# A hybrid encoder layer on one core: V's tiles at multiples of 64 bytes, the last row pair by halves in fresh banks, four reciprocals behind a weight chunk's low parts

## The chip, the cores and the metric

The kernel runs on one core of one Trainium2 chip. The metric is the device time of one execution in microseconds (us); the time before is 630.35 us, the median of 3 runs (630.19 to 630.4). Engines in the profile: PE (TensorE, matmuls), PEld (its weight loads), DVE (VectorE), ACT (ScalarE), POOL (GpSimd) and SP, which here only issues transfers. A q behind an engine's name (SPq, ACTq) means its sequencer, with the transfers it issues.

## The reference

One layer of a bidirectional encoder, 512 tokens of 2048 features: a combined input projection, attention (8 heads of 128, 2 key/value heads, axial rotary embedding) beside a gated linear recurrence in both directions, both normed and gated, and one output projection with the residual.

```
h = rms_norm(x, norm_w)
proj = jnp.einsum('bsd,de->bse', h, w_in)
q, k, v, g_attn, xr, g_lru = jnp.split(proj, SPLITS, axis=-1)
attn_out = attention_group(q, k, v, q_norm_w, k_norm_w)
lru_out = lru_group(xr, conv_w, conv_b, lru_wa, lru_ba, lru_wx, lru_bx, lru_lambda)
mixed = jnp.concatenate([rms_norm(attn_out, attn_norm_w) * jax.nn.silu(g_attn),
                         rms_norm(lru_out, lru_norm_w) * jax.nn.silu(g_lru)], axis=-1)
return x + jnp.einsum('bse,ed->bsd', mixed, w_out)
```

## The kernel before

**Products in three parts.** Every operand of a matmul is split into a high part (a rounded copy, fp32r) and a low part (what is left), and a product is three matmuls: high by high, high by low, low by high (`mm3`, L152 to L155, and `product`, L1029, for the output projection). ScalarE makes the high parts (for weights L218), VectorE the low parts (L219). So each 256-row chunk of the input projection's weights (`wload`, L224) comes through a ring of three raw buffers, and gives two pairs of high and low tiles, k = 0 and 1, of 128x512. `wsplit` (L211) numbers the chunks in `turn_of` and keeps, in `split_done`, the two instructions (the copy, the subtraction) of the chunk's k = 1 under the chunk's number. A chunk is used by 24 matmuls: four output blocks, each two k by three.

**Order.** TensorE's order is written out by hand. For the other engines most of the program is ordered by a planner, by priority (`tc.high_priority`), its own estimate of when things are ready, and the edges that the program gives it: `tc.issue_after(ins)`, wrapped in `behind(those)` (L243), puts an instruction behind another on the same engine. SP is ordered by hand in the attention stage, and all four other engines are in the output projection (`outputs`).

**V and attention.** `kv` (L654) takes keys and values from the projection. For each of 4 token blocks one V tile holds the high and the low part, 256 columns each (2 heads of 128). The tile is made by `aside` (L863): it is 16 columns of 4 bytes longer than needed, 2112 bytes per partition, and V begins 8 columns (32 bytes) in. V's parts are the stationary operand of `values` (L731): 12 matmuls per head, with the softmax weights (tiles ph and pl) as moving operand. There are eight heads.

**The norm's reciprocals.** `spread` (L827) sums squares over partitions by two matmuls with ones, ScalarE takes the square root into `gbc`, and VectorE inverts it in place in four pieces of 128 columns (L835). It is called twice: for the recurrence (from `kv`) and for attention (from `later`, L1351, after the first two output blocks of the last input projection, with high priority). That last projection takes its chunks by `take` (L1300), which fetches one chunk more and hands over the oldest of those fetched; three are fetched ahead.

**The output projection.** It uses a form of Strassen's method with seven products of half-size blocks, named P1, Q5, Q6, Q7, Q3, P2, Q4, for each half g of the output columns, each a sum over NP = 8 steps i. `product(dst, i, k, b, n)` adds step i to the two PSUM banks dst[0] and dst[1], one for each block of 128 rows (s), in six matmuls of 512 columns. The last three products (Q3, P2, Q4) run together; in the second half their last two steps are drawn apart at the end, L1139: first both steps of Q3, then of P2, then of Q4, and after each product `last` (L1060) adds its two banks to the result tiles xt and cb in SBUF (VectorE, L1066) and sends the rows out (L1058). For the very last product, Q4, the second row block's add is cut into two halves, the first sent by ScalarE's queue, the second by SP's. In the loop over i before it, `feed` issues loads and splits of the output weights for later steps, on VectorE among others, and `residual` (L1103) adds x (L1112).

Of the kernel before, what the change touches and what calls it, by code (L numbers as in the profile page):

```python
# [12 lines left out]
F32R = mybir.dt.float32r  # L13
# [4 lines left out]
P = 128  # L18
SEQ = 512
DM = 2048  # L20
KT = DM // P
NT = SEQ // P
HD = 128
NH = 8
NKV = 2
# [23 lines left out]
H = 256  # L49
# [14 lines left out]
def hybrid_kernel(  # L64
# [53 lines left out]
    def nm(s):  # L118
        cnt[0] += 1
        return f"{s}_{cnt[0]}"  # L120
# [19 lines left out]
    def pj():  # L140
        return ps.tile([P, SEQ], F32, tag="pj", name=nm("pj"))
# [101 lines left out]
    def behind(those):  # L243
        stack = ExitStack()
        for ins in those:
            stack.enter_context(tc.issue_after(ins))
        return stack
# [406 lines left out]
    def kv(es):  # L654
        turned_k = sent(norm_rope(es, NKV, rk), NKV)
        yield 20
        opened("wx", "right")
        for t in range(NT):
            vv = es[t][:, NKV * HD :]
            vt = aside(  # L660
                lambda *a: pools["qkv"].tile(*a, tag="v", bufs=NT, name=nm("v")), 2 * NKV * HD // H
            )
            vh[t], vl[t] = vt[:, 0, :], vt[:, 1, :]
            nc.scalar.copy(vh[t], vv)
            nc.vector.tensor_sub(vl[t], vv, f(vh[t]))
        yield from lru_squares()
        yield 2
        drain(turned_k)
        yield 6
        pair = landed(asides.pop(0))  # L670
        for h in range(NKV):
            yield (12, 4)[h]
            kt = pools["qkv"].tile([P, 2, SEQ], F32R, tag="kt", bufs=NKV, name=nm("kt"))
            kth[h], ktl[h] = kt[:, 0, :], kt[:, 1, :]
            those = split_head(pair, h, kth[h], ktl[h])
        parts = halved(
            sums["l"],
            lambda: pools["rope"].tile([P, SEQ], F32R, tag="kv", bufs=NT, name=nm("kv")),
            those,
        )  # L680
        yield 4
        spread(gbc, parts, NB * P)
# [141 lines left out]
            nc.vector.tensor_sub(lo, src, f(hi))  # L824
        return hi, lo

    def spread(dst, parts, n):  # L827

        pb = mm()
        for k, part in enumerate(parts):  # L830
            nc.tensor.matmul(pb, ones_r, part, start=k == 0, stop=k == 1)  # L831
        nc.scalar.activation(dst, pb, AF.Sqrt, scale=1.0 / n, bias=eps[:, :1])
        for t in range(NT):
            ts_ = slice(t * P, (t + 1) * P)
            nc.vector.reciprocal(dst[:, ts_], dst[:, ts_])  # L835

    gbc = const([P, SEQ], "gbc")

# [12 lines left out]
    def seven(pair, hi, lo):  # L851
# [7 lines left out]
        for to, part in ((slice(0, 3), src[:, 1:4]), (slice(3, 7), res)):  # L859
            nc.scalar.copy(hi[:, to], part)  # L860
            nc.vector.tensor_sub(lo[:, to], part, f(hi[:, to]))

    def aside(tile_of, n):  # L863

        t = tile_of([P, n * H + 16], F32R)
        return t[:, 8 : 8 + n * H].rearrange("p (n e) -> p n e", e=H)

    def kept(pool, i):
        return [
# [144 lines left out]
    def outputs(work):  # L1014

        order = [(g, n, i) for g in range(2) for n in range(2) for i in range(NP)]
        feeds, parts = [], []  # L1020
        for g, n, i in order:
            parts.append([])
            feeds.append((feed1, feed2)[n](g, i, parts[-1]))

        def feed(u):
            if u < len(feeds):
                next(feeds[u])

        def product(dst, i, k, b, n):  # L1029
            ah, al = (t[:, k] for t in mixed[i][1])  # L1030
            bh, bl = (t[:, n] for t in b)
            for s in range(2):
                ts_ = slice(s * P, (s + 1) * P)
                for j, (lh, rh) in enumerate(((ah, bh), (ah, bl), (al, bh))):
                    nc.tensor.matmul(  # L1035
                        dst[s], lh[:, ts_], rh, start=i == 0 and j == 0, stop=i == 7 and j == 2
                    )

        def banks(*kinds):
            return [[kind() for _ in range(2)] for kind in kinds]  # L1040

        with tc.high_priority(SOON):
            for u in (0, 1, 0, 0, 1):
                feed(u)
        next(work)
        feed(1)
        next(work)
        feed(2)
        for g in range(2):

            xs = [
                pools["out"].tile([P, NT, SEQ], F32, tag=t, bufs=1, name=nm(t))
                for t in ("xt", "cb")
            ]

            def leave(t, j, queue, e0=0, e1=SEQ):
                c0 = (2 * g + j) * SEQ
                queue.dma_start(of[tokens[t], c0 + e0 : c0 + e1], xs[j][:, t, e0:e1])  # L1058

            def last(t0, j, acc, cut=1):  # L1060
                for s in range(2):
                    n = cut if s else 1
                    for e0 in range(0, SEQ, SEQ // n):
                        e1 = e0 + SEQ // n
                        to = xs[j][:, t0 + s, e0:e1]
                        nc.vector.tensor_add(to, to, acc[s][:, e0:e1])  # L1066
                        queue = nc.scalar if e1 < SEQ else nc.sync
                        leave(t0 + s, j, queue if g else nc.gpsimd, e0, e1)

            p1, q5, q6, q7 = banks(*((mm, mm, pj, pj), (pj, mm, mm, pj))[g])  # L1070
            for i in range(NP):
                u = 16 * g + i
                xb, yb = parts[u]
                product(p1, i, P1, xb, 1)
                if i < NP - 1:
                    product(q5, i, Q5, xb, 0)
                    next(work, None)
                    feed(u + 2)
                    product(q6, i, Q6, yb, 0)
                    product(q7, i, Q7, yb, 1)  # L1080
                    feed(u + 2)
                    feed(u + 3)
                    continue

                for s in range(2):
                    nc.scalar.copy(xs[1][:, 2 + s], p1[s])
                product(q6, i, Q6, yb, 0)
                for s in range(2):
                    nc.vector.tensor_sub(xs[1][:, s], xs[1][:, 2 + s], q6[s])
                product(q5, i, Q5, xb, 0)  # L1090
                for s in range(2):
                    nc.vector.tensor_sub(xs[0][:, 2 + s], q5[s], xs[1][:, s])
                feed(u + 2)
                product(q7, i, Q7, yb, 1)
                for s in range(2):
                    nc.vector.tensor_add(xs[0][:, s], q7[s], xs[0][:, 2 + s])
                feed(u + 2)
                for s in range(2):
                    nc.vector.tensor_sub(xs[1][:, s], xs[1][:, s], q7[s])
                feed(u + 3)  # L1100


            def residual(m, j):  # L1103
                xr = in_av() if g else in_fin("t4", 2, 2)
                c0 = (2 * g + j) * SEQ
                nc.gpsimd.dma_start(
                    xr,
                    xf[2 * m * P : 2 * (m + 1) * P, c0 : c0 + SEQ].rearrange("(t p) e -> p t e", p=P),
                )
                yield  # L1110
                to = xs[j][:, 2 * m : 2 * m + 2]
                nc.vector.tensor_add(to, to, xr)  # L1112
                if (m, j) == (0, 0):
                    for t in range(2):
                        leave(t, 0, nc.gpsimd)
                yield

            rs = [residual(n // 2, n % 2) for n in range(4)]
            next(rs[0]), next(rs[1])
            q3, p2, q4 = banks(*((mm, mm, pj), (pj, mm, mm))[g])  # L1120
            takes = ((q3, Q3, 0, 0), (p2, P2, 0, 1), (q4, Q4, 1, 0))
            ends = ((2, 0), (2, 1), (0, 1))
            added = (2, 3, 4, 5) if g else (2, 3, 5, 6)
            for i in range(NP - 2 * g):
                u = 16 * g + NP + i
                for (dst, k, b, n), (t0, j) in zip(takes, ends):
                    product(dst, i, k, parts[u][b], n)
                    if i == NP - 1:
                        last(t0, j, dst)
                    if k == P2:  # L1130
                        if i in added:
                            next(rs[added.index(i)])
                        if i in (2, 3):
                            next(rs[i])
                        feed(u + 2)
                feed(u + 2)
                feed(u + 3)

        for (dst, k, b, n), (t0, j) in zip(takes, ends):  # L1139
            for i in (NP - 2, NP - 1):  # L1140
                product(dst, i, k, parts[24 + i][b], n)
            last(t0, j, dst, 2 if k == Q4 else 1)

# [205 lines left out]
    def later():  # L1351
# [1 line left out]
            parts = halved(sums["a"], lambda: fin_s(dt=F32R))  # L1353
        yield 2
        with tc.high_priority():
            spread(gbc, parts, NH * HD)
        yield 4
        for pair in ap_[:2]:
            normed(pair)
# [86 lines left out]
```

## Time and profile before

| | |
|---|---|
| median of 3 runs | 630.35 us |
| the profiled execution's own time | 630.30 us |
| its span, first to last instruction | 628.2 us |
| granted TensorE clock | 0.999 |
| matmuls, and their weight loads | 2755 each |
| DMA, mean over the span | 203 GB/s |

The profile's tables give for a group: line, engine, operation, out<-in tiles, shape, count, then busy time in us, mean of one in ns, and idle time before. The timeline gives the start in us, the time taken in us, engine, line, operation, tiles, shape and count (several in a row are merged). A wait row says who waited for whom: total us, how often, longest. Matmuls overlap: one is recorded for about 0.39 us, but the next starts 0.23 us after it, and it is the distance of starts that sets the time.

### The profile page before, as it was taken

The numbers are of one execution on the slowest core, as the hardware profiler recorded it, in microseconds if no ns is written. First come the engines' busy times: TensorE is split into PE (matmuls) and PEld (weight loads), VectorE is DVE, ScalarE is ACT, GpSimd is POOL, SyncE is SP. The second block draws the span as 40 slices with busy tenths as digits, with TensorE's granted clock in tenths as the row PEclk, the third lists the DMA queues.
The fourth block names the chain that finished last, engine by engine and source line by source line (L and its number), as shares of the span: only waits on it lengthen the run. The fifth ranks groups of instructions, "written<-read, shape, count | busy, mean of one in ns | idle before, by whom it ended". The sixth has DMA issues, their size and how long they took to land.

```text
span 628.2 us, 8273 instructions
## 1 busy us (share of the span) xinstructions
PE 622.0 (99%) x2755; PEld 512.5 (82%) x2755; DVE 494.6 (79%) x794; ACT 353.1 (56%) x618; POOL 101.4 (16%) x134
## 2 busy tenths in 40 slices
PE   9999999999999999999999999999999999999997
PEld 7888888888888888888888888887888888888885
DVE  5958979986699875987887888549978866886885
ACT  3674899379946823555475447438436643444441
POOL 0000210112002622522122232100120101110010
PEclk9999999999999999999999999999999999999999
DMA  8878785859774599479668646922996777896252
GB/s 284 281 209 263 176 202 172 176 134 192 237 234 135 172 255 227 109 214 267 183 170 254 194 150 185 268 69 67 280 232 204 224 254 244 287 340 213 68 201 100
DMA packets 73594, 127.61 MB, mean 203 GB/s; under 512 B 6616, under 2 KB 29264, under 8 KB 73552
## 3 DMA queue, kind: packets, MB, share of 16 engines
q1 hardware_dynamic: 65664, 109.65, 55.9%
q0 software_dynamic: 7712, 17.31, 14.2%
q8 instruction: 21, 0.34, 0.2%
q14 instruction: 21, 0.17, 0.1%
q10 hardware_dynamic: 176, 0.14, 0.1%
HBM read 110.29 MB, written 37.75 MB: 236 GB/s over the span
## 4 chain that ended last, share of the span: by engine, by line
PE 98%; DVE 1%; issue 0%; DVEq 0%; POOL 0%; POOLq 0%
PE pj L155 20%; PE pj L153 20%; PE pj L154 20%; PE mm L1035 14%; PE pj L1035 10%; PE mm L155 4%; PE mm L153 3%; PE mm L154 3%; PE pj L388 1%; PE mm L253 1%; PE mm L1153 1%; DVE gbc L835 1%; DVE wl L219 0%; DVE cb L1066 0%; PE mm L831 0%
## 5 line engine op out<-in xcount | busy, mean ns | idle before, releaser
L155 PE MATMUL pj<-x,wl 128*128 128x512 f32 x376 | 146.8, 390 | 0.4 <-DVE wl L219 0.3
L153 PE MATMUL pj<-x,wh 128*128 128x512 f32 x376 | 147.0, 391 | 0.0
L154 PE MATMUL pj<-x,wh 128*128 128x512 f32 x376 | 146.6, 390 | 0.0
L218 ACT CAST wh<-wr 128x512 fp32r<-128x512 f32 x143 | 85.4, 617 | 81.9 <-PE pj L154 32.0
L219 DVE TENSOR_TENSOR wl<-wr,wh 128x512 fp32r<-128x512 f32 x144 | 100.0, 724 | 21.2 <-ACT wh L218 19.9
L887 ACT CAST wh<-wr 128x1024 fp32r<-128x1024 f32 (+1 forms) x72 | 60.5, 860 | 77.3 <-PE mm L1035 35.9
L888 DVE TENSOR_TENSOR wl<-wr,wh 128x1024 fp32r<-128x1024 f32 (+1 forms) x72 | 68.5, 985 | 30.7 <-ACT wh L887 30.5
L155 PEld LDWEIGHTS pj<-x,wl 128*128 128x128 f32 x376 | 70.6, 188 | 16.1 <-DVE wl L219 1.3
L153 PEld LDWEIGHTS pj<-x,wh 128*128 128x128 f32 x376 | 70.6, 188 | 14.7
L154 PEld LDWEIGHTS pj<-x,wh 128*128 128x128 f32 x376 | 70.6, 188 | 14.7
L153 PE MATMUL pj<-wh,x 128*128 128x512 f32 x192 | 74.8, 389 | 0.0
L155 PE MATMUL pj<-wh,x 128*128 128x512 f32 x192 | 74.8, 389 | 0.0
L154 PE MATMUL pj<-wl,x 128*128 128x512 f32 x192 | 74.8, 389 | 0.0
L911 POOL DMA_DIRECT2D t<-in_w_out_dram x40 | 33.5, 901 | 161.3 <-DMA t<-in_w_out_dram 99.5
L1035 PE MATMUL mm<-wl,mh 128*128 128x512 f32 x128 | 49.8, 389 | 0.0
L1035 PE MATMUL mm<-wh,mh 128*128 128x512 f32 x128 | 49.8, 389 | 0.0
L1035 PE MATMUL mm<-wh,ml 128*128 128x512 f32 x128 | 49.8, 389 | 0.0
L153 PEld LDWEIGHTS pj<-wh,x 128*128 128x128 f32 x192 | 36.0, 188 | 7.5
L154 PEld LDWEIGHTS pj<-wl,x 128*128 128x128 f32 x192 | 36.0, 188 | 7.5
L155 PEld LDWEIGHTS pj<-wh,x 128*128 128x128 f32 x192 | 36.0, 188 | 7.4
L708 POOL TENSOR_SCALAR p<-p,sm 128x512 f32<-128x512 f32 x32 | 24.3, 764 | 90.0 <-DVE sm L707 90.0
L1035 PE MATMUL pj<-wh,mh 128*128 128x512 f32 x96 | 37.4, 390 | 0.0
(200 smaller groups left out, 1038.2 us busy)
## 6 DMA issues: line engine op xcount, KB each, us to landing
wr<-in_w_in_dram SPq DMA_DIRECT2D x71, 512.0 KB, 5.1
wr<-in_w_out_dram SPq DMA_DIRECT2D x24, 512.0 KB, 5.1
t<-in_w_out_dram POOLq DMA_DIRECT2D x40, 256.0 KB, 6.8
wr<-t SPq DMA_DIRECT2D x40, 256.0 KB, 5.9
pd<-u SPq DMA_DIRECT2D x16, 512.0 KB, 3.0
pt<-pd SPq DMA_DIRECT2D x64, 128.0 KB, 3.9
t<-in_w_out_dram SPq DMA_DIRECT2D x24, 256.0 KB, 5.5
t<-t SPq DMA_DIRECT2D x16, 256.0 KB, 5.7
```

The costliest lines, as they stand in the source:

```text
L153: nc.tensor.matmul(acc, lh, rh, start=start, stop=False)
L154: nc.tensor.matmul(acc, lh, rl, start=False, stop=False)
L155: nc.tensor.matmul(acc, ll, rh, start=False, stop=stop)
L218: copy(hi, raw[:, k, :]).ins,
L219: nc.vector.tensor_sub(lo, raw[:, k, :], f(hi)).ins,
L253: nc.tensor.transpose(pt[:, t * P : (t + 1) * P], xc[:, t, ks], ident)
L388: nc.tensor.matmul(acc[e], w[:, e * P : (e + 1) * P], x_[k], start=k == 0 and j == 0, stop=False,)
L708: last_pool[0] = nc.gpsimd.tensor_scalar(p, p, sm, 0.0, op0=ALU.mult, op1=ALU.add).ins
L887: nc.scalar.copy(hi[:, to], b)
L888: nc.vector.tensor_sub(lo[:, to], b, f(hi[:, to]))
L911: nc.gpsimd.dma_start(dst, src, accum_op=ALU.add)
L1035: nc.tensor.matmul(dst[s], lh[:, ts_], rh, start=i == 0 and j == 0, stop=i == 7 and j == 2)
```

## The change

Three edits.

V's tile is allocated as [128, 2, 256] directly; `aside` goes. So each V tile is 2048 bytes per partition instead of 2112, and V starts where the tile starts.

`spread` takes a list `those`, and each of its four reciprocals is put behind these instructions on VectorE. The second call hands over the k = 1 subtraction of the chunk that was fetched last but one; the first call hands over nothing.

In the output projection's second half, Q4's sum for the second row block is closed after step 5 (NP - 3), and VectorE adds it to the result there (one more add of 128x512). The two last steps then run in another order: first both steps for the first row block, its add and its transfer; then, in two newly taken PSUM banks, both steps for columns 0 to 255 of the second row block, with add and transfer, and both steps for columns 256 to 511, with add and transfer. Twelve matmuls of 256 columns take the place of six of 512; the weight loads of the second row block are made twice.

```diff
         for t in range(NT):
             vv = es[t][:, NKV * HD :]
-            vt = aside(
-                lambda *a: pools["qkv"].tile(*a, tag="v", bufs=NT, name=nm("v")), 2 * NKV * HD // H
-            )
+            vt = pools["qkv"].tile([P, 2, NKV * HD], F32R, tag="v", bufs=NT, name=nm("v"))
             vh[t], vl[t] = vt[:, 0, :], vt[:, 1, :]
...
-    def spread(dst, parts, n):
+    def spread(dst, parts, n, those=()):
...
-            nc.vector.reciprocal(dst[:, ts_], dst[:, ts_])
+            with behind(those):
+                nc.vector.reciprocal(dst[:, ts_], dst[:, ts_])
...
-        def product(dst, i, k, b, n):
+        def product(dst, i, k, b, n, ss=range(2), es=slice(None), ends_=(0, NP - 1)):
             ah, al = (t[:, k] for t in mixed[i][1])
             bh, bl = (t[:, n] for t in b)
-            for s in range(2):
+            for s in ss:
                 ts_ = slice(s * P, (s + 1) * P)
                 for j, (lh, rh) in enumerate(((ah, bh), (ah, bl), (al, bh))):
                     nc.tensor.matmul(
-                        dst[s], lh[:, ts_], rh, start=i == 0 and j == 0, stop=i == 7 and j == 2
+                        dst[s][:, es], lh[:, ts_], rh[:, es],
+                        start=i == ends_[0] and j == 0, stop=i == ends_[1] and j == 2,
                     )
...
-            def last(t0, j, acc, cut=1):
-                for s in range(2):
-                    n = cut if s else 1
-                    for e0 in range(0, SEQ, SEQ // n):
-                        e1 = e0 + SEQ // n
-                        to = xs[j][:, t0 + s, e0:e1]
-                        nc.vector.tensor_add(to, to, acc[s][:, e0:e1])
-                        queue = nc.scalar if e1 < SEQ else nc.sync
-                        leave(t0 + s, j, queue if g else nc.gpsimd, e0, e1)
+            def last(t0, j, acc, ss=range(2), e0=0, e1=SEQ):
+                for s in ss:
+                    to = xs[j][:, t0 + s, e0:e1]
+                    nc.vector.tensor_add(to, to, acc[s][:, e0:e1])
+                    queue = nc.scalar if e1 < SEQ else nc.sync
+                    leave(t0 + s, j, queue if g else nc.gpsimd, e0, e1)
...
                 for (dst, k, b, n), (t0, j) in zip(takes, ends):
-                    product(dst, i, k, parts[u][b], n)
+                    if g and i == NP - 3 and k == Q4:
+                        product(dst, i, k, parts[u][b], n, (0,))
+                        product(dst, i, k, parts[u][b], n, (1,), ends_=(0, i))
+                        nc.vector.tensor_add(xs[j][:, t0 + 1], xs[j][:, t0 + 1], dst[1])
+                    else:
+                        product(dst, i, k, parts[u][b], n)
...
         for (dst, k, b, n), (t0, j) in zip(takes, ends):
-            for i in (NP - 2, NP - 1):
-                product(dst, i, k, parts[24 + i][b], n)
-            last(t0, j, dst, 2 if k == Q4 else 1)
+            pieces = [(dst, (0, 1), 0, SEQ, (0, NP - 1))]
+            if k == Q4:
+                pieces = [(dst, (0,), 0, SEQ, (0, NP - 1))] + [
+                    ((None, pj()), (1,), e0, e0 + H, (NP - 2, NP - 1)) for e0 in (0, H)
+                ]
+            for to, ss, e0, e1, ends_ in pieces:
+                for i in (NP - 2, NP - 1):
+                    product(to, i, k, parts[24 + i][b], n, ss, slice(e0, e1), ends_)
+                last(t0, j, to, ss, e0, e1)
...
         with tc.high_priority():
-            spread(gbc, parts, NH * HD)
+            spread(gbc, parts, NH * HD, split_done[turn_of[0] - 2][1:])
```

More of the change, by code (lines that the diff above doesn't have):

```diff
@@ L861, in seven @@
             nc.vector.tensor_sub(lo[:, to], part, f(hi[:, to]))
-    def aside(tile_of, n):
-        t = tile_of([P, n * H + 16], F32R)
-        return t[:, 8 : 8 + n * H].rearrange("p (n e) -> p n e", e=H)
     def kept(pool, i):
```

## The prediction

> **What bounds the kernel now.** I read the page first (engine table, chain, clock row), then TensorE's waits, then the timeline at the one place where it waits late, at V's matmuls and over the last 15 us.
>
> ```profile
> span 628.2 us, 8273 instructions
> PE 622.0 (99%) x2755; PEld 512.5 (82%) x2755; DVE 494.6 (79%) x794; ACT 353.1 (56%) x618; POOL 101.4 (16%) x134
> PEclk9999999999999999999999999999999999999999
> PE 98%; DVE 1%; issue 0%; DVEq 0%; POOL 0%; POOLq 0%
> L153 PE MATMUL mm<-kt,q 128*128 128x512 f32 x32 | 12.5, 389 | 0.0
> L153 PE MATMUL mm<-ph,v 128*128 128x512 f32 x32 | 12.7, 397 | 0.0
> PE pj L155 <- DVE wl L219: 0.3, 1, 0.3
> ```
>
> TensorE is busy 99% at full clock and is 98% of the chain; everything else has its cover. A change can only win where TensorE loses cadence or stands still, and after its last matmul. In a steady stretch 21 matmuls of 512 columns take 4.78 us (row at 618.12 below), 0.2267 us each by the finer spacing of neighbouring starts. The change touches one place of each kind: V's matmuls (mean 397 ns where others show 389), the only late wait of TensorE, and the tail.
>
> **The change part by part.** All sums start from the profiled execution's own 630.30 us: a span of 628.2 and 2.1 around it. The median of the runs, 630.35, is practically the same.
>
> *V's tiles.* Two blocks of V, the first and the last of eight (32 matmuls of a kind, four per head):
>
> ```profile
> 300.77 0.40 PE L155 MATMUL mm<-kt,q 128*128 128x512 f32 x1
> 301.01 0.39 PE L153 MATMUL mm<-ph,v 128*128 128x512 f32 x1
> 305.65 0.39 PE L155 MATMUL pj<-x,wl 128*128 128x512 f32 x1
> 416.53 0.40 PE L155 MATMUL pj<-x,wl 128*128 128x512 f32 x1
> 421.41 0.39 PE L155 MATMUL pj<-x,wl 128*128 128x512 f32 x1
> ```
>
> From the matmul during which V's first weights are loaded to the place where the old cadence is back are 21 matmuls: 12 with V as weights, one before and eight behind. They take 305.65 - 300.77 = 4.88 us, and 421.41 - 416.53 = 4.88 again, where 21 x 0.2267 = 4.76. So a block loses 0.12 us, and eight lose 0.95. The two blocks agree though different work stands before them (kt,q; pj), so the loss belongs to the V block. In the code, V is the one weight operand that begins 32 bytes inside its tile; the program's memory plan puts every other matmul operand of 128 or 512 columns at a multiple of 64 bytes. The change puts V there too. No run shows V at another address, so the gain lies between nothing and 0.95. I take **-0.95**, since the only operand placed differently is the one that is slow, in all its uses. The edit itself adds no instruction: the same four casts and four subtractions, 256 bytes less in all, so tiles allocated below V move by 256 bytes, which keeps them at multiples of 64.
>
> The Trainium skill ("SBUF — State Buffer", Specifications) speaks against this: it gives SBUF lines of 16 bytes, so a start at 32 bytes is already on a whole line, and by it the move is worth nothing. No run so far separates the two; what it would make of the sum is the first rival.
>
> *The second reciprocal.*
>
> ```profile
> 426.40 0.39 PE L153 MATMUL pj<-x,wh 128*128 128x512 f32 x1
> 432.24 1.13 ACT L218 CAST wh<-wr 128x512 fp32r<-128x512 f32 x2
> 433.85 0.95 DVE L861 TENSOR_TENSOR ml<-hs,mh 128x768 fp32r<-128x768 f32 x1
> 434.71 3.39 DVE L835 RECIPROCAL gbc<-gbc 128x128 f32<-128x128 f32 x4
> 437.98 0.39 PE L154 MATMUL pj<-x,wh 128*128 128x512 f32 x1
> 438.01 2.43 DVE L219 TENSOR_TENSOR wl<-wr,wh 128x512 fp32r<-128x512 f32 x4
> 438.70 0.50 PE L155 MATMUL pj<-x,wl 128*128 128x512 f32 x1 [0.33 <-DVE wl L219]
> 441.58 0.39 PE L155 MATMUL pj<-x,wl 128*128 128x512 f32 x1
> 444.30 0.39 PE L155 MATMUL pj<-x,wl 128*128 128x512 f32 x1
> 445.97 1.23 DVE L840 TENSOR_TENSOR av<-av,gbc 128x1024 f32<-128x1024 f32 x1
> ```
>
> The high parts of a weight chunk were ready at 433.4, but VectorE ran four reciprocals first, and the chunk's low parts came at 438.7. TensorE needed the first at 438.21 and stood; from 437.98 to 441.58 are 13 matmuls, 3.60 us against 13 x 0.2267 = 2.95. So the place costs 0.65: 0.49 of standing and the rest in slow cadence behind it. Counting chunks: when the reciprocals are written into the program, the chunk last fetched is the fourth of this projection; two back in the numbering means the third, and its second low part is what they are pinned behind. That is the chunk of the stall (chunks of 24 matmuls, 5.44 us, after the projection's start at 426.40; the two matmuls of the sums lie in between). The order becomes: two low parts from 434.8 to 436.1, ahead of 438.21; then reciprocals until 439.5; then the next chunk's two low parts, until 440.4 as before, where TensorE first asks for one at 444.30. The work on VectorE is the same, only exchanged. Late next is the reciprocals' result, 439.5 instead of 438.0, with its first reader at 445.97. The weights' raw buffers come free some 3 us earlier, which only helps SP's loads. **-0.65**; bounds 0 (the planner lets another piece of work take the place) and 0.65.
>
> *The last row pair.*
>
> ```profile
> 613.93 1.22 DVE L1112 TENSOR_TENSOR cb<-cb,wr 128x1024 f32<-128x1024 f32 x1
> 615.21 1.83 DVE L888 TENSOR_TENSOR wl<-wr,wh 128x1024 fp32r<-128x1024 f32 x2
> 617.48 1.37 DVE L1066 TENSOR_TENSOR xt<-xt,pj 128x512 f32<-128x512 f32 x2 [0.44 <-PE pj L1035]
> 618.12 4.78 PE mm L1035 x21
> 620.20 1.37 DVE L1066 TENSOR_TENSOR cb<-cb,mm 128x512 f32<-128x512 f32 x2 [1.35 <-PE mm L1035]
> 622.92 1.43 DVE L1066 TENSOR_TENSOR cb<-cb,mm 128x512 f32<-128x512 f32 x3 [1.35 <-PE mm L1035]
> 623.17 0.39 PE L1035 MATMUL mm<-wh,ml 128*128 128x512 f32 x1
> L1066 DVE TENSOR_TENSOR cb<-cb,mm 128x256 f32<-128x256 f32 x2 | 0.8, 418 | 0.0
> 623.93 0.41 DVE L1066 TENSOR_TENSOR cb<-cb,mm 128x256 f32<-128x256 f32 x1
> 624.05 0.37 ACTq L1058 DMA_DIRECT2D out_dram<-cb  x1
> 624.38 0.33 SPq L1058 DMA_DIRECT2D out_dram<-cb  x1
> GB/s 282 328 109 0 0 0 0 73 391 355 401 346 328 319 118 0 0 0 0 64 355 382 364 342 310 332 178 5 0 0 0 0 0 0 0 0 0 0 0 0
> out_dram<-cb SPq DMA_DIRECT2D x1, 128.0 KB, 2.7
> 15.78 1.03 PE L253 MATMUL mm<-ident,b 128*128 128x128 f32 x8
> L253 PE MATMUL mm<-ident,b 128*128 128x128 f32 x40 | 5.8, 287 | 0.0
> ```
>
> (The GB/s row is of the window 620 to 629, slices of 0.225 us.) Today the last adds run behind each other: the first row block at 622.92 for 0.69, two halves of 0.42, out at 624.35; the final transfer is issued at 624.38. The DMA engines are busy without a gap from slice 19 (about 624.4) to slice 26 (626.1): three transfers, 512 KB together, the last of them queued behind the other two.
>
> The change adds one VectorE add of 128x512 (0.69) in the sixth step. It stands between the two subtractions of 615.21, and waits for matmuls that end about 615.6, before its turn at 616.43. Behind it the second subtraction ends at 617.8 instead of 617.1; TensorE wants that result only at about 621.4. The two adds of 617.48 start about 0.3 late, their transfers too, and the idle 1.35 before 620.20 takes that up: nothing on the path. Cover gone, it would be 0.69.
>
> The last 12 matmuls start at 623.17 - 11 x 0.227 = 620.68. New order: six for the first row block, the last starting at 621.81 and ending at 622.20; its add 622.24 to 622.93. Then twelve of 256 columns in place of six of 512. No row has that shape. Below: half of 0.227, 0.113. Above: 0.227, no shrinking. Nearest are the eight transposes, a weight load with 128 columns each: (1.03 - 0.29) / 7 = 0.106 us, 0.29 being the mean length of one. Loading weights so fits under 0.113, and I take 0.12. The first half ends about 622.92 and is added until 623.35, the second ends at 623.64, is added by 624.09 and issued at 624.12: 0.26 earlier. From issue to first byte today's first block takes some 0.8 us (added by 623.61, bytes from slice 19 on); at 624.12 + 0.8 = 624.9 the earlier two transfers, moved forward by 0.6 to 0.7, are through, so it also saves the queueing of some 0.45 (624.38 + 0.8 = 625.2 against a start about 625.65). **-0.70**. Bounds: -0.77 at 0.113; -0.26 if landing stays 2.7 after the issue; +0.57 if the halves stay at 0.227 each (1.28 later at the add, less what was saved).
>
> Sum: 630.30 - 0.95 - 0.65 - 0.70 = **628.0**.
>
> **The rivals.**
>
> *V's start doesn't matter.* The cadence also slows behind aligned operands:
>
> ```profile
> 429.12 0.62 PE L831 MATMUL mm<-s,ones_r 128*128 128x512 f32 x2
> 430.73 0.39 PE L155 MATMUL pj<-x,wl 128*128 128x512 f32 x1
> ```
>
> From 429.12 are seven matmuls in 1.61 us, where 7 x 0.2267 = 1.59. If the V blocks' loss comes from their waits or from p as moving operand, it stays: 630.30 - 1.35 = 628.95. Against it: this place costs 0.02 to 0.03, a V block four times that. It would also be the outcome by the skill's 16-byte lines.
>
> *The stall only moves.* The planner that orders VectorE puts other waiting work (the 1.22 and 0.95 subtractions of the build) before the two low parts, enough to be late by as much: more than the 2.1 us between 436.1 and 438.2. Then -0.65 is lost: 628.65.
>
> *Halves as slow as wholes.* 630.30 - 0.95 - 0.65 + 0.57 = 629.27, within the bound below. The transposes at 0.106 speak against it.
>
> *Slower: a new plan.* Outside the last stage the planner orders VectorE and ScalarE anew, from the moved V tiles (which lie on memory of earlier tiles, and so wait for others) and the new edges on. Place: the weights' low parts from 190 to 470 us. Price: 0.65 for each chunk late, as at 438. Up to three such stalls leave the time between 628.65 and 629.95; four are needed to eat 2.30, and six give 630.30 - 2.30 + 3.90 = 631.9. For it: VectorE is busy 79%, more in these stretches. Against it: the present plan has one wait of this kind after the start (0.3 in the waits row), and the edges are in one place.
>
> **How the numbers follow.** A measurement here can tell 0.2%, 1.26 us, from no change: faster is under 629.09, slower over 631.61. All as forecast, 628.0: 0.56. V worth nothing, 628.95: 0.14. Stall moved, 628.65: 0.07. These three are faster: 0.77. Halves not shrinking, 629.27: 0.06, and a new plan with two or three stalls, about 629.6: 0.09, make "same" 0.15. The slower plan, 631.9: 0.08. The range from 627.4 (all at their best bound, and half a microsecond of slow cadence elsewhere that goes as well) to 629.4 holds the first four, 0.83.
>
> **What would show it.** V's matmuls at a mean of 389 to 391 instead of 394 to 397, and 4.76 us over the same 21; if they stay, the first rival holds. The row of TensorE waiting for L219 gone, reciprocals from about 436; a wait elsewhere on wl names the moved stall. Twelve matmuls of 128x256 over 1.36 to 1.45 us, the last issue 0.2 to 0.3 closer to TensorE's end than now (the 1.2 from 623.17 to 624.38). New idle on TensorE between 190 and 470 would make the prediction wrong.

## The result, and the profile after

| | before | after |
|---|---|---|
| median of 6 runs | 630.28 us (629.92 to 630.4) | 627.57 us (627.17 to 628.09) |
| span of the profiled execution | 628.2 us | 625.6 us |
| own time of the profiled execution | 630.30 us | 627.43 us |

The ratio is 0.9958, 95% interval 0.9946 to 0.9971: 2.7 us faster, more than the 0.2% that can be told from no change. The forecast was 628.0.

The page of the kernel after (span, engines, clock, chain):

```profile
span 625.6 us, 8287 instructions
PE 620.6 (99%) x2761; PEld 513.1 (82%) x2761; DVE 494.3 (79%) x795; ACT 353.1 (56%) x618; POOL 101.6 (16%) x134
PEclk9999999999999999999999999999999999999999
PE 99%; DVE 0%; issue 0%; POOL 0%; POOLq 0%
```

Six matmuls more and 1.4 us less of busy TensorE: what TensorE gained is cadence and standing time, not work. The rest of the gain lies behind its last matmul. The table of TensorE's waits no longer has the row of L219; what is left of it is the start:

```profile
PE mm L1156 <- POOL ones L161: 1.1, 1, 1.1
```

V's matmuls, in the table of groups (last number but one the mean in ns):

```profile
L153 PE MATMUL mm<-ph,v 128*128 128x512 f32 x32 | 12.5, 390 | 0.0
```

The first V block in the timeline, from its first start to the start of the 21st behind it:

```profile
300.42 0.39 PE L155 MATMUL mm<-kt,q 128*128 128x512 f32 x1
300.65 0.39 PE L153 MATMUL mm<-ph,v 128*128 128x512 f32 x1
...
305.18 0.39 PE L155 MATMUL pj<-x,wl 128*128 128x512 f32 x1
```

The mean went from 397 to 390 ns, and the same 21 matmuls take 305.18 - 300.42 = 4.76 us instead of 4.88.

VectorE around the second reciprocal, and TensorE's matmul that used to wait:

```profile
433.48 1.28 DVE L219 TENSOR_TENSOR wl<-wr,wh 128x512 fp32r<-128x512 f32 x2
434.68 3.38 DVE L834 RECIPROCAL gbc<-gbc 128x128 f32<-128x128 f32 x4
437.98 1.22 DVE L219 TENSOR_TENSOR wl<-wr,wh 128x512 fp32r<-128x512 f32 x2
...
436.71 0.39 PE L154 MATMUL pj<-x,wh 128*128 128x512 f32 x1
436.93 0.39 PE L155 MATMUL pj<-x,wl 128*128 128x512 f32 x1
437.16 0.39 PE L153 MATMUL pj<-x,wh 128*128 128x512 f32 x1
```

Two low parts, four reciprocals, two low parts: TensorE goes from 436.71 to 436.93 without a stop where it stood 0.49 us before.

The tail in the timeline (VectorE's adds, TensorE's last pieces, the last issue):

```profile
613.28 1.23 DVE L882 TENSOR_TENSOR wl<-wr,wh 128x1024 fp32r<-128x1024 f32 x1
614.43 0.68 DVE L1122 TENSOR_TENSOR cb<-cb,mm 128x512 f32<-128x512 f32 x1
615.02 0.69 DVE L882 TENSOR_TENSOR wl<-wr,wh 128x512 fp32r<-128x512 f32 x1
615.63 1.29 DVE L1058 TENSOR_TENSOR xt<-xt,pj 128x512 f32<-128x512 f32 x2
618.27 1.37 DVE L1058 TENSOR_TENSOR cb<-cb,mm 128x512 f32<-128x512 f32 x2 [1.35 <-PE mm L1029]
...
620.11 0.28 PE L1029 MATMUL pj<-wh,mh 128*128 128x256 f32 x1
621.42 0.28 PE L1029 MATMUL pj<-wh,ml 128*128 128x256 f32 x1
...
621.74 0.42 DVE L1058 TENSOR_TENSOR cb<-cb,pj 128x256 f32<-128x256 f32 x1 [0.30 <-PE pj L1029]
622.19 0.33 SPq L1053 DMA_DIRECT2D out_dram<-cb  x1
```

The last transfer in the table of issues (size, us from issue to landing):

```profile
out_dram<-cb SPq DMA_DIRECT2D x1, 128.0 KB, 2.3
```

Eleven distances from 620.11 to 621.42 make 0.119 us for a matmul of 256 columns. The early add (L1122) sits between the two subtractions, and the idle 1.35 before 618.27 is as long as before, so it costs nothing. From the end of the last matmul to the end of the span it is now 625.6 - 621.7 = 3.9 us; before it was 628.2 - 623.56 = 4.6.

**Where the 2.60 us of span went.** Matching TensorE's matmuls one by one in the two traces, the lead grows in four places: 0.35 in the first 50 us, 0.93 over the eight V blocks (0.12 each, but 0.09 for one that took 4.79), 0.65 at the reciprocals, and 0.67 in the tail (0.75 less after TensorE's end, 0.08 more on TensorE). The first of these is none of the change's: the kernel before stood 0.3 us for a low part at the start, where the change has no instruction. Those rows of before:

```profile
43.17 0.39 PE L154 MATMUL pj<-x,wh 128*128 128x512 f32 x1
43.66 0.50 PE L155 MATMUL pj<-x,wl 128*128 128x512 f32 x1
```

In other executions this stall is missing or lies elsewhere: the single edits below are the kernel before up to that point; two show none of that size, and the third one at 48.87. So a span from one execution carries some tenths of a microsecond from the start, and the three terms are read from their places.

### The profile page after: what moved, and what is told of

Its sections match the earlier page's. It is cut to its first block, busy times and chain, and to the rows that moved or that the text cites. A ratio compares the mean times of both kernels' runs of the same rounds, so it can differ in the third digit from the quotient of the medians.

```text
span 625.6 us, 8287 instructions
## 1 busy us (share of the span) xinstructions
PE 620.6 (99%) x2761; PEld 513.1 (82%) x2761; DVE 494.3 (79%) x795; ACT 353.1 (56%) x618; POOL 101.6 (16%) x134
## 4 chain that ended last, share of the span: by engine, by line
PE 99%; DVE 0%; issue 0%; POOL 0%; POOLq 0%
PE pj L153 21%; PE pj L155 21%; PE pj L154 21%; PE mm L1029 14%; PE pj L1029 11%; PE mm L155 3%; PE mm L153 3%; PE mm L154 3%; PE pj L388 1%; PE mm L253 1%; PE mm L1156 1%; PE mm L829 0%; PE mm L367 0%; DVE cb L1058 0%; PE mm L189 0%
## 5 line engine op out<-in xcount | busy, mean ns | idle before, releaser
L219 DVE TENSOR_TENSOR wl<-wr,wh 128x512 fp32r<-128x512 f32 x144 | 99.6, 720 | 21.3 <-ACT wh L218 20.2
L1029 PE MATMUL pj<-wl,mh 128*128 128x512 f32 (+1 forms) x100 | 38.5, 385 | 0.0
```

Of the source, the lines that this page charges most:

```text
L219: nc.vector.tensor_sub(lo, raw[:, k, :], f(hi)).ins,
L1029: nc.tensor.matmul(dst[s][:, es], lh[:, ts_], rh[:, es], start=i == ends_[0] and j == 0, stop=i == ends_[1] and j == 2,)
```

## The experiments

Times are medians; the kernel before ran on the same chip and in the same rounds (medians 630.27 to 630.29). The ratio to it, with its 95% interval, goes by all runs, so it is not exactly the quotient of two medians.

| run | median us | ratio |
|---|---|---|
| v_only | 629.17 | 0.9983 (0.9974 to 0.9992) |
| recip_only | 629.54 | 0.9989 (0.9980 to 0.9998) |
| tail_only | 629.09 | 0.9981 (0.9972 to 0.9990) |
| weights_aside | 638.48 | 1.0131 (1.0117 to 1.0144) |
| weights_64b | 635.95 | 1.0090 (1.0076 to 1.0104) |
| weights_16b | 637.60 | 1.0114 (1.0099 to 1.0130) |
| rows_only | 627.98 | 0.9963 (0.9951 to 0.9976) |
| begin12 | 629.59 | 0.9999 (0.9990 to 1.0008) |
| all_by_64 | 627.40 | 0.9956 (0.9944 to 0.9969) |
| v_64_of_2304 | 628.32 | 0.9968 (0.9955 to 0.9980) |
| v_128_of_2304 | 628.41 | 0.9970 (0.9958 to 0.9982) |
| ones_moved | 627.60 | 0.9955 (0.9941 to 0.9969) |

### Each edit alone

v_only is the kernel before with the V line of the diff; recip_only the kernel before with `those` handed to the second `spread`; tail_only is the change with the other two undone (V's tiles 2112 bytes long again, and V 32 bytes in).

> The kernel before with V's tiles moved alone. Theory (V's start 32 bytes in slows the cadence): each of eight V blocks goes from 4.88 to 4.76 us, TensorE's end comes 0.95 us earlier, time 0.9 to 1.0 under before (ratio about 0.9985); the stall at 438 and the tail stay. Rival (start doesn't matter, the blocks' loss comes from waits or from the moving operand): 4.88 us stays and the time is before's within 0.2.

> The kernel before with the reciprocals' pin alone. Theory: TensorE's only late wait on the low parts near 438 goes, 0.65 us (ratio about 0.9990); V blocks stay 4.88, the tail stays. Rival (the stall only moves, or the edges make a new plan): a wait on low parts elsewhere, time as before within 0.2.

> The change with V's start and the pin undone, so the last row pair alone. Theory: 12 matmuls of 256 columns at 0.12 us, 0.08 longer on TensorE, last issue 0.2 to 0.3 earlier, end 0.7 us earlier (ratio about 0.9989). Rival (landing takes as long from the issue as before): 0.26 earlier.

Each is faster on its own, by 1.1, 0.7 and 1.2 us; the sum, 3.0, agrees with the whole 2.7 within the intervals of about half a microsecond each. The traces are sharper. With V alone a block, from 300.33 to 305.10, takes 4.77 us, as two rows of its timeline show:

```profile
300.33 0.39 PE L155 MATMUL mm<-kt,q 128*128 128x512 f32 x1
305.10 0.39 PE L155 MATMUL pj<-x,wl 128*128 128x512 f32 x1
```

Its waits still have the stall on low parts:

```profile
PE pj L155 <- DVE wl L219: 0.4, 1, 0.4
```

With the reciprocals held back alone (recip_only) the waits table has no such row, and TensorE stands for low parts nowhere else after the start: the stall went and did not move. With the tail alone, TensorE's last matmul starts at 623.50 of a span of 627.6, as far from the end as in the change, and its last transfer lands 2.3 us after its issue, not 2.7. So each edit brings its own gain. The rivals "the stall only moves", "halves as slow as wholes" and "landing takes as long from the issue as before" fall. So does "V's start doesn't matter"; what it is about V's start that matters isn't settled by v_only, which changes both the 32 bytes and the length of the tiles.

### The suspected cost taken twelvefold: weights 32, 64 and 16 bytes in

```diff
-        hi = pool.tile([P, SEQ], F32R, tag="wh", bufs=4, name=nm("wh"))
-        lo = pool.tile([P, SEQ], F32R, tag="wl", bufs=4, name=nm("wl"))
+        hi, lo = (
+            pool.tile([P, SEQ + 16], F32R, tag=t, bufs=4, name=nm(t))[:, 8 : 8 + SEQ]
+            for t in ("wh", "wl")
+        )
```

weights_64b begins at column 16 of the same tiles, weights_16b at column 4.

> The change, with the high and low tiles of all chunks of the input projection's weights begun 32 bytes inside tiles 64 bytes longer. Theory that a weight (stationary) operand 32 bytes in costs 5.7 ns a matmul: the 1128 matmuls with these tiles as stationary operand go from a distance of 0.2267 to 0.2325, 6 to 6.5 us slower than the change, so about 634; the 576 matmuls that have these tiles as moving operand stay at 0.2267. If a moving operand counts as well: 3.3 us more, about 637. Rival (the start doesn't matter): 627.6.

> As the run before with the weights' tiles 64 bytes longer, but begun 64 bytes in instead of 32. Theory (what counts is the start within 64 bytes): cadence 0.2267 again, time as the change's, 627.2 to 628.1. Rival (the longer tiles, or where the other tiles come to lie, made the 638.5): 638 again.

> The same tiles begun 16 bytes in. If any start off a multiple of 64 bytes costs (a row of 64 bytes more to read per partition): 637 to 640, as at 32 bytes. If only the half, 32 bytes, counts, or a start at a multiple of 16 is free: 627.6.

The first came out 10.9 us over the change, more than either estimate: the mean distance of these matmuls is 0.232 to 0.233 us, about what the theory said for weights and moving operands together, and others behind them are slow too. Groups of weights_aside (stationary: pj<-x,wh; moving: pj<-wh,x; not touched: mm<-wh,mh):

```profile
L153 PE MATMUL pj<-x,wh 128*128 128x512 f32 x376 | 148.7, 395 | 0.0
L153 PE MATMUL pj<-wh,x 128*128 128x512 f32 x192 | 75.9, 395 | 0.0
L1031 PE MATMUL mm<-wh,mh 128*128 128x512 f32 x126 | 49.0, 389 | 0.0
```

So the operand's place counts when it is the moving operand as well as when it is the weights. In the moving groups the weights (x) all lie where they lay in the change, so it isn't only the step from one set of weights to the next. But then weights_64b, 64 bytes in, is slow too, and my theory falls: a multiple of 64 is not enough. Its groups:

```profile
L153 PE MATMUL pj<-x,wh 128*128 128x512 f32 x376 | 148.2, 394 | 0.0
L153 PE MATMUL pj<-wh,x 128*128 128x512 f32 x192 | 75.5, 393 | 0.0
L1031 PE MATMUL mm<-wh,mh 128*128 128x512 f32 x126 | 49.0, 389 | 0.0
```

weights_16b, 16 bytes in, is slow as well: 637.60, means of 393 to 396 ns. A cost of any start off a multiple of 64 would look like this too, but weights_64b rules that reading out.

I then took every matmul's two operands from the program's memory plan and set the distance to the next matmul beside them. In the change both operands of every matmul of 512 columns start at 192 modulo 256 bytes, except in the six that have the ones as weights. Tiles of 2112 bytes start 64 bytes further each: in the kernel before V began at 224, 32, 96 and 160 modulo 256, in weights_64b the weights begin at 0, 64, 128 and 192. The pairs that differ modulo 256 were slow in all these runs (mean distance 0.231 to 0.235 us by groups); in the change, pairs that differ by odd multiples of 256 are not (0.2267). A quarter of the weight tiles in weights_64b do lie at 192, and their matmuls are 0.230 to 0.233 us apart all the same; misplaced ones stand a few matmuls before and behind them, so this run alone doesn't give the rule. That made a new theory, that moving operand and weights have to start at the same place modulo 256, with rivals: the place itself (192), or a period of 64 or 128.

### The same place modulo 256

```diff
+    const([P, 16], "gap")
     ident = const([P, P], "ident")
...
-    opened("pad", "right").tile([P, 8], F32, name="pad")
+    opened("pad", "right").tile([P, 56], F32, name="pad")
```

(all_by_64.) For V alone, in the change, with columns 16 to 528 (v_64_of_2304) or 32 to 544 (v_128_of_2304):

```diff
-            vt = pools["qkv"].tile([P, 2, NKV * HD], F32R, tag="v", bufs=NT, name=nm("v"))
+            vt = pools["qkv"].tile([P, 576], F32R, tag="v", bufs=NT, name=nm("v"))
+            vt = vt[:, 16 : 528].rearrange("p (n e) -> p n e", e=H)
```

> The change with every SBUF tile moved by 64 bytes (modulo 256): by the memory plan all moving and stationary operands of 512 and 128 columns then start at 0 modulo 256, where in the change they all start at 192; ones stays 64 apart from the rest. Theory R (what counts is that moving operand, weights and the next weights start at the same place modulo 256): cadence 0.2267, time as the change's, 627 to 628. Theory A (the place itself counts): distances of 0.231 to 0.233 everywhere, 638 or more.

> The change with V's tiles 2304 bytes long (9 x 256) and V begun 64 bytes in: V is at a multiple of 64 bytes, at 0 modulo 256 where all other operands are at 192. Multiples of 64 suffice: 4.76 us per V block, the change's time. Same place modulo 256 counts: about 4.85 to 4.88 per block, 0.7 to 0.95 over the change.

> The same tiles with V begun 128 bytes in, 64 modulo 256. If the period is 128: 4.76 us per V block, the change's time. If it is 256: about 4.85 to 4.88, 0.7 to 0.95 over the change.

The first V block in all_by_64, then in v_64_of_2304, then in v_128_of_2304, from a matmul to the 21st behind it:

```profile
300.58 0.39 PE L154 MATMUL mm<-kt,q 128*128 128x512 f32 x1
305.34 0.39 PE L154 MATMUL pj<-x,wh 128*128 128x512 f32 x1
```

```profile
300.24 0.39 PE L155 MATMUL mm<-kt,q 128*128 128x512 f32 x1
305.11 0.39 PE L155 MATMUL pj<-x,wl 128*128 128x512 f32 x1
```

```profile
300.45 0.40 PE L155 MATMUL mm<-kt,q 128*128 128x512 f32 x1
305.33 0.39 PE L155 MATMUL pj<-x,wl 128*128 128x512 f32 x1
```

4.76, 4.87 and 4.88 us. Everything moved together to 0 keeps the full cadence (627.40), so the place itself doesn't count; V at a multiple of 64 that lies 64 from the rest, and even at one that lies 128 from it, loses what it lost 32 bytes in (0.75 and 0.84 over the change by the medians, 0.9 by the traces). Period 64 and period 128 fall. What in the chip has this period wasn't tried.

### Ones and identity to the same place

```diff
+    const([P, 16], "gap")
     ident = const([P, P], "ident")
...
+    const([P, 48], "gap2")
     nhalf = const([P, 48], "nhalf")
```

> The change with the ones and the identity, the last operands off the common place, moved to 192 modulo 256 as all others. If the same place counts: the 0.02 to 0.03 us of slow cadence behind each of the three sums over partitions go (L829 near 236 and 428, L367 near 50), under 0.1 us in all, less than the time can tell. If their cadence stays, those places have another cause.

The last sum over partitions in the timeline of the change, then of ones_moved, each to the seventh matmul behind its first:

```profile
427.84 0.62 PE L829 MATMUL mm<-s,ones_r 128*128 128x512 f32 x2
429.45 0.39 PE L155 MATMUL pj<-x,wl 128*128 128x512 f32 x1
```

```profile
428.24 0.61 PE L831 MATMUL mm<-s,ones_r 128*128 128x512 f32 x2
429.82 0.39 PE L155 MATMUL pj<-x,wl 128*128 128x512 f32 x1
```

1.61 becomes 1.58, and the other two sums do the same: the row that I had set against V's start in the prediction had the same cause as V. In the time it can't be told (627.60).

### The tail without halves

```diff
-                pieces = [(dst, (0,), 0, SEQ, (0, NP - 1))] + [
-                    ((None, pj()), (1,), e0, e0 + H, (NP - 2, NP - 1)) for e0 in (0, H)
-                ]
+                pieces = [
+                    (dst, (0,), 0, SEQ, (0, NP - 1)),
+                    ((None, pj()), (1,), 0, SEQ, (NP - 2, NP - 1)),
+                ]
```

The second row block's add is still cut in halves.

> The change, but the second row block's last six matmuls stay 512 columns wide in one new bank, and its add is in two halves at the end: the row order and the early add alone. Theory (the end is the last add plus the queue behind it): TensorE ends 0.08 earlier than the change, the last issue comes 0.3 later than the change's relative to TensorE's end, as in the kernel before, but the first row block's transfer is out of the way; time 0.2 to 0.4 over the change's 627.57. Rival (halves bring nothing, the earlier first transfer is all): the change's time.

Its last matmul and the two last adds in the timeline:

```profile
621.60 0.39 PE L1029 MATMUL pj<-wh,ml 128*128 128x512 f32 x1
622.02 0.75 DVE L1058 TENSOR_TENSOR cb<-cb,pj 128x256 f32<-128x256 f32 x2 [0.67 <-PE pj L1029]
```

Its span, from the page:

```profile
span 626.1 us, 8276 instructions
```

From TensorE's end to the span's it is 626.1 - 622.0 = 4.1 us, against 4.6 in the kernel before and 3.9 in the change. So of the 0.75 some 0.5 comes from the row order alone, which clears the first transfer out of the way and leaves the last adds as late as they were, and some 0.25 from the halves, which cost 0.08 on TensorE: 0.2 net. The medians say 0.41. Of the 0.5 between the two spans, 0.4 is there already at 52 us, in the start of the execution; how much of it the medians hold isn't known. The rival, that halves bring nothing, falls by the trace; by the times alone it stays open.

### Attention one step later

`BEGIN` 12 instead of 11 in the change.

> The change with attention begun one step later (BEGIN 12), aimed at TensorE's weight load that waits 0.1 us for the first head's queries near 266. If the queries are merely late by less than one step of 1.4 us: that wait and its slow cadence go, 0.17 us; if the later start makes another wait at attention's end, none or worse.

A miss. The small wait near 266 went, but the softmax weights of the first head came late. TensorE's waits (sum, count, longest):

```profile
PE mm L154 <- DVE pl L726: 1.4, 1, 1.4
```

The granted clock (the number ahead of the DMA share, which the GB/s follow) in some stretches of 1 us:

```profile
304.00:305.00 1.00, 0.45 (x2) 0.41 (x3) 1.00 (x2) 0.00 (x0) 0.00 (x0) 1.00 0.97 213
305.00:306.00 1.00, 1.00 (x5) 0.76 (x4) 1.00 (x3) 0.00 (x0) 0.00 (x0) 0.60 0.94 336
306.00:307.00 1.00, 1.00 (x4) 0.81 (x3) 1.00 (x3) 0.02 (x1) 0.00 (x0) 0.50 0.04 14
307.00:308.00 1.00, 1.00 (x3) 0.73 (x3) 0.49 (x1) 1.00 (x3) 0.00 (x0) 0.50 0.00 0
308.00:309.00 1.00, 1.00 (x5) 0.80 (x4) 0.04 (x1) 0.43 (x2) 0.00 (x0) 0.69 0.00 0
309.00:310.00 1.00, 1.00 (x6) 0.84 (x5) 0.78 (x3) 0.32 (x1) 0.19 (x1) 1.00 0.00 0
```

A wait of 1.4 us was followed by some 3 us at half clock, and the block lost 3.7 us in all. That execution took 631.58 us, with a mean clock of 0.997. Of the 11 runs it and three more are long (630.86 to 631.58, all at 0.997); the other seven took 629.32 to 629.79 at 0.999 or 1.0. So the median, 629.59, is 2.0 over the change, which is about the wait alone, and the lost clock comes on top in some executions. The ratio to the kernel before is 0.9999. Why the clock falls only in some of them isn't shown: only one was traced.

No run beats the change by more than the measurement can tell.

## Why the prediction was right

**What bounds the kernel.** Right: TensorE is 98% of the chain before and 99% after, and all of the gain that the trace shows lies at the three places named, but for the 0.35 at the start.

**V, -0.95.** Right in size (0.93 by the trace, and 1.11 with 0.6 either way by the time), wrong in the reason. The step that failed is the cause: "the only operand placed differently is the one that is slow" was read as 32 bytes inside its tile, with a multiple of 64 bytes as the cure. What counts is that moving operand and weights start at the same place modulo 256, shown by the four V placements and the move of everything. With tiles of 2048 bytes V came to lie at 192 like the rest; at 0 or at 64, both multiples of 64, it loses 0.9 (v_64_of_2304, v_128_of_2304). So that the change put it right was luck. The remark that moving tiles by 256 bytes is harmless was right by the same luck: 256 is the period. The Trainium skill's line size of 16 bytes ("SBUF — State Buffer", Specifications), by which the move was worth nothing, does not account for this cost: the move was worth 0.93, and V and the weights at other multiples of 16 were slow.

**The reciprocals, -0.65.** Right: the order on VectorE came out as written, piece by piece, the stall went and none took its place.

**The tail, -0.70.** Right: -0.67. The 256-column matmul was taken at 0.12 and measured 0.119; issue to landing fell from 2.7 to 2.3 us, some 0.4 where 0.45 of queueing had been put. The row that the last issue would come 0.2 to 0.3 nearer to TensorE's last start was mis-stated: 622.19 - 621.42 = 0.77 against 1.21, that is 0.44 nearer, as the prediction's own times say (issue at 624.12, last start at 621.81 + 0.227 + 11 x 0.12 = 623.36); 0.26 was the distance to the old issue. The early add was put at a delay of 0.3 for the adds behind it. It was less: against 617.48, less the 1.93 that TensorE was ahead there, they start at 615.63, 0.08 late.

**The rivals.** A new plan with stalls didn't come: outside the two late places the plan's work is where it was. begin12 shows that it could have: one step's shift brought a wait that cost 2.0 us by the medians, and 3.7, more than all three edits won, in the execution that was traced.

**The sum, 628.0.** Measured 627.57. The trace's three terms make 2.25, the medians 2.71; the rest is within the interval (1.8 to 3.4 us), and the start of an execution can make tenths of it. Whether anything of it is the change's stays open.

## What to carry to other kernels

Where matmuls run back to back, read the distance of their starts, not only the waits: a loss of 6 ns in each never shows as a wait. Lay out moving operands and weights so that they start at the same place modulo 256 bytes (shown here for fp32r matmuls of 512 columns), and count every padding (a 64-byte tail on a tile moves all that follow it). At the end of a kernel, order the last work so that large transfers leave first and the last piece is small, and price it down to the transfer's queue.

## What the runs showed of the hardware

A matmul of 512 columns (fp32r) whose weights and moving operand don't start at the same place modulo 256 bytes is followed 4 to 8 ns late (distance 0.231 to 0.235 us instead of 0.2267). The full cadence comes back only some matmuls later: in the kernel before, the eight distances behind a V block still average 0.2315 us, and then it is 0.2267 again. It makes no difference which of the two operands is moved away (means of 395 ns either way in weights_aside). What in the chip has this period isn't known from these runs. Weight loads of 128 columns nearly fit under matmuls of 256 (0.119 us each, where half of 0.2267 is 0.113). A wait of TensorE of 1.4 us inside a dense stretch can be followed by some 3 us at half the granted clock (begin12, in the traced execution).
